# A hybrid retention and delta-rule layer on one core: weights split into high and low parts once and kept in DRAM

## The chip, the cores and the metric

The kernel runs on one core of a Trainium2 chip. Its engines are TensorE (PE, matrix products), VectorE (DVE), ScalarE (ACT), GpSimd (POOL) and SyncE (SP, which issues most of the DMAs). The metric is the device time of one execution in microseconds, as the median of three runs.

## The reference

One layer over 2048 new prompt tokens and 64 sample tokens, with a model width of 1024, in float32. The mixer has four retention heads and four gated delta heads that share one input projection and one output projection; the MLP is a squared ReLU, 4096 wide.

```python
def _layer(x, pos_offset, s_ret, s_gdn, s_conv, pre_mix_w, w_in, ...):
    h = _rmsnorm(x, pre_mix_w)
    m, S_r, S_g, new_conv = _hybrid_mixer(h, pos_offset, s_ret, s_gdn, s_conv, w_in, conv_w, ...)
    x = x + _rmsnorm(m, post_mix_w)
    h = _rmsnorm(x, pre_mlp_w)
    f = jnp.square(jax.nn.relu(jnp.einsum('bld,df->blf', h, w_up)))
    f = jnp.einsum('blf,fd->bld', f, w_down)
    x = x + _rmsnorm(f, post_mlp_w)
    return x, S_r, S_g, new_conv
```

Inside the mixer each head is a recurrence over chunks. For a delta head the kernel inverts a triangular 128 x 128 matrix per chunk, block by block.

## The kernel before

The 2048 prompt tokens go through as four blocks of 512; the 64 sample tokens go along with the second block. Each block has a projection stage (16 units of weights), the heads, an output projection (4 units of `w_out`), and an MLP in eight groups of two units of `w_up` and two of `w_down`. The weights do not stay in SBUF: every block reads all of them from DRAM, 52 units of four pieces, so 208 pieces a block and 832 in all. A piece is 128 partitions x 512 numbers, 256 KB (264 KB for `w_vg0`).

A float32 product is made from three products of a rounded 32-bit form that PE runs fast: high x high, high x low, low x high. So each piece is split after its load (`load_unit`, L339 to L354): ACT copies it into the rounded form (`whi`, through the helper at L248), and DVE or POOL subtracts this from the original (`wlo`, helper L254). The tuple `pool=(1, 1, 0, 0)` gives the first two pieces of a unit to POOL and the last two to DVE. There are five buffers `wraw` for raw pieces (RB) and six each for `whi` and `wlo` (WB); a buffer is used again in turn when its last reader is done.

There are two kinds of products. In `gemm_fm` (projections, `w_up`) the weights are the stationary operand, and a unit is passed through once for each of its two column groups. In `gemm_tm` (`w_vg`, `w_out`, `w_down`) the tokens are stationary, and a unit is passed through once for each of the four tiles of 128 tokens. In `w_out` the contraction goes in the order 0, 4, 1, 5, 2, 6, 3, 7 of the heads' outputs.

The order of work on PE is written by the program: a class (`Weave`) interleaves the main stream of products with side streams, such as the heads, from a table of assumed latencies, and PE keeps that order. From the second block on, the projections of a block are woven together with the MLP of the block before it; the last block's MLP runs alone at the end. On the other engines and on SP's queue, a scheduler sets the order when the program is built. Each engine, and SP's queue of DMAs too, takes its instructions strictly in order.

A delta head sends parts of its matrix through small DMAs on SP's queue: `XX<-ym` and `ym<-ym` (L789, L782, L783) before the inversion of the 16 x 16 blocks, `ym<-xf` (L808 to L811) after it, and `ym<-ym` (L824) after the joining of pairs of blocks. Each waits for DVE.

Of the kernel before, what the change touches and what calls it, by code (L numbers as in the profile page):

```python
# [8 lines left out]
F32 = mybir.dt.float32  # L9
F32R = mybir.dt.float32r  # L10
# [18 lines left out]
NF = 4  # L29
# [92 lines left out]
class Weave:  # L122
    """Interleaves the main stream of matrix products with side streams whose
    steps wait on other engines; keeps an estimate of the tensor engine's clock."""
# [54 lines left out]
    def merge(self, *gens):  # L179
        """Units of the streams given, the earlier stream first where it is ready.  # L180
        A stream yields a tuple of keys before each unit, and None within it."""
        todo = [[next(g), g] for g in gens]
        while todo:
            for e in todo:
                if self.ready(e[0]):
                    break
            else:
                yield [e[0] for e in todo]
                continue
            while True:  # L190
                try:
                    x = next(e[1])
                except StopIteration:
                    todo.remove(e)
                    break
                if isinstance(x, tuple):
                    e[0] = x
                    break
                yield x
# [3 lines left out]
def hybrid_kernel(ctx: ExitStack, tc: tile.TileContext, I, O, NB: int, SB: int):  # L203
# [13 lines left out]
    mmp = ctx.enter_context(tc.tile_pool(name="mmp", bufs=MMB, space=PS))  # L217
    drp = ctx.enter_context(tc.tile_pool(name="drp", bufs=2, space=bass.MemoryType.DRAM))
# [53 lines left out]
    # ---- constants  # L272
# [65 lines left out]
    # ---- weights: streamed pieces, split into hi + lo  # L338
    def load_unit(src, n, ncol):  # L339
        """src: [128, n, ncol] in DRAM; returns accessors k -> AP [128, ncol] for hi and lo."""  # L340
        per = 2 if ncol <= NU else 1
        his, los = [], []
        for q in range(n // per):
            fit = lambda t: t[:, :per * ncol].rearrange("p (a c) -> p a c", a=per)
            r = fit(page([P, 2 * NU], "wraw", bufs=RB))
            nc.sync.dma_start(r, src[:, per * q:per * (q + 1), :])
            hi = fit(page([P, 2 * NU], "whi", F32R, bufs=WB))
            lo = fit(page([P, 2 * NU], "wlo", F32R, bufs=WB))
            act(hi, r, AF.Copy)
            tt(lo, r, hi.bitcast(F32), ALU.subtract, eng=(V, G)[TUNE["pool"][q % 4]])  # L350
            his.append(hi)
            los.append(lo)
        return (lambda k: his[k // per][:, k % per, :]), (lambda k: los[k // per][:, k % per, :])

    def gemm_tm(ps, a, wu, c0, rows, ks, first=True, last=True):
        """ps[rows, :] (+)= a[:, ks, c0:c0+rows]^T W[ks], in three passes."""
        ahi, alo = a
        whi, wlo = wu
        ks = list(ks)
        for n, k in enumerate(ks):  # L360
            lh, ll = ahi[:, k, c0:c0 + rows], alo[:, k, c0:c0 + rows]
            matmul(ps, lh, whi(k), start=(first and n == 0), stop=False)
            matmul(ps, lh, wlo(k), start=False, stop=False)
            matmul(ps, ll, whi(k), start=False, stop=(last and n == len(ks) - 1))
            if n % 2 == 1:
                yield

    def gemm_samp(wd, a, wu):
        """Sample rows of a, times W: rows of the high parts, then rows of the low parts, added up."""
        ps = mm()  # L370
        whi, wlo = wu
        for k in range(KT):
            both = a[0][:, k, T:T + 2 * NS]
            matmul(ps[:, :wd], both, whi(k), start=(k == 0), stop=False)
            matmul(ps[:, :wd], both, wlo(k), start=False, stop=(k == KT - 1))
            if k % 2 == 1:
                yield
        x = page([P, 512], "fs")[:NS, :wd]
        V.tensor_copy(x, ps[NS:2 * NS, :wd])
        tt(x, x, ps[:NS, :wd], ALU.add)  # L380
        return x

    def gemm_fm(ps, a, wu, m, n0, n1):
        """ps[128, n1-n0] = W[:, 128m:128m+128]^T a[:, :, n0:n1]."""
        ahi, alo = a
        whi, wlo = wu
        for k in range(KT):
            wh, wl = whi(k)[:, m * P:(m + 1) * P], wlo(k)[:, m * P:(m + 1) * P]
            matmul(ps, wh, ahi[:, k, n0:n1], start=(k == 0), stop=False)
            matmul(ps, wh, alo[:, k, n0:n1], start=False, stop=False)  # L390
            matmul(ps, wl, ahi[:, k, n0:n1], start=False, stop=(k == KT - 1))
            yield
# [4 lines left out]
    class Block:  # L397
# [23 lines left out]
        # ------------ input norm  # L421
        def place(self):
            """high and low parts; with the sample rows, their low parts once more behind the high ones"""
# [3 lines left out]
        def prep_first(self):  # L427
# [15 lines left out]
            self.w0 = load_unit(I["w_vg0"], KT, NU)  # L443
# [80 lines left out]
        # ------------ mixer output: kept in DRAM until the operand's place is free  # L524
# [33 lines left out]
        # ------------ gates of the delta heads  # L558
# [70 lines left out]
        # ------------ gated delta heads  # L629
        def conv_channel(self, ct, pss, out, outs, raws):  # L630
            """pre-conv projections in PSUM -> silu(conv) in out [128, T] and outs [128, NS]."""
# [38 lines left out]
        def spare(self, i, h):  # L670
            """places that only the first block has, for its odd heads"""
# [6 lines left out]
        def proj_qk(self, h):  # L678
            kq = self.spare(0, h) or page([P, 2, T], "kq", bufs=2)
            kqs = small([P, 2, NS], "kqs") if self.samp else None  # L680
            wu = load_unit(I["w_qk"][h], KT, UNIT)
# [5 lines left out]
        def proj_vz(self, h):  # L687
            vz = self.spare(1, h) or page([P, 2, T], "Ss" if self.b == 0 and h else "vz")
            vzs = small([P, 2, NS], "vzs") if self.samp else None
            wu = load_unit(I["w_vz"][h], KT, UNIT)  # L690
# [16 lines left out]
        def gdn_head(self, h):  # L707
# [12 lines left out]
            # decay matrix  # L720
# [7 lines left out]
            # token-major k and q  # L728
# [33 lines left out]
            # (k k^T o D)^T | (q k^T o D)^T, rows weighted by c  # L762
# [6 lines left out]
            # diagonal blocks of 16: one block a partition, rows of the inverse in turn  # L769
# [35 lines left out]
            # pairs of blocks: (T1^T M21^T) T2^T, four rows a partition, zero for the second block's  # L805
# [25 lines left out]
            # token-major v  # L831
# [5 lines left out]
            # T = (I + M C)^-1 by doubling  # L837
# [18 lines left out]
            # recurrence over chunks  # L856
# [148 lines left out]
        # ------------ retention heads  # L1005
# [8 lines left out]
        def ret_place(self, h):  # L1014
            """four places of [P, 1024]; the first one is free before the others are"""
# [7 lines left out]
        def proj_vg(self, h):  # L1023
# [3 lines left out]
            if h == 0 and b == 0:  # L1027
                wu = self.w0
            else:
                wu = load_unit(I["w_vg0"] if h == 0 else I["w_ret"][h, 1], KT, wd)  # L1030
# [26 lines left out]
        def proj_ret(self, h):  # L1057
# [4 lines left out]
            wu = load_unit(I["w_ret"][h, 0], KT, UNIT)  # L1062
# [99 lines left out]
        # ------------ mixer  # L1162
# [46 lines left out]
        # ------------ output projection, residual, second norm  # L1209
        def out_proj(self, then=None):  # L1210
# [17 lines left out]
            for u in range(4):  # L1228
                wu = load_unit(I["w_out"][u], KT, UNIT)
# [66 lines left out]
        # ------------ MLP  # L1296
# [17 lines left out]
        def mlp_up(self, g):  # L1314
            self.f = f = (page([P, NF, T], "fhi", F32R), page([P, NF, T], "flo", F32R),
                          page([P, NF, 2, NS], "fs", F32R) if self.samp else None)
            for u in range(NF // 2):
                if u:
                    yield ()
                wu = load_unit(I["w_up"][g * (NF // 2) + u], KT, UNIT)  # L1320
# [11 lines left out]
        def mlp_down(self, g, then=None):  # L1332
            if g == 0:
                self.acc = [page([P, D_MODEL], atag[t]) for t in range(self.nt)]
            for u in range(2):
                if u and g < NG - 1:
                    yield ()
                whi, wlo = wu = load_unit(I["w_down"][g, u], NF, T)
# [7 lines left out]
                for t, (c0, rows) in enumerate(self.tiles):  # L1346
# [6 lines left out]
                    else:  # L1353
                        # rows of the high parts, then rows of the low parts; added up at the end
# [162 lines left out]
```

## Time and profile before

| | |
|---|---|
| runs | 3055.93, 3059.34 and 3065.72 us |
| median | 3059.34 us |
| span of the profiled execution | 3047.0 us, the only time of it that is given |
| busy, share of the span | PE 94%, DVE 61%, ACT 38%, POOL 34% |
| mean granted TensorE clock | 0.979 |
| moved by DMA | 317.82 MB, 104 GB/s on the mean |

The profile is one execution. An engine's busy time says how much work it has; whether this work sets the end is said by the waits, which name for each stretch of idleness the instruction that ended it. Numbers such as "31.9, 21, 3.9" in a wait are the time in total, the number of waits, and the longest.

### The profile page before, as it was taken

To read this page: it belongs to the slowest core of one execution; us is meant where nothing else is said; L and a number is where in the kernel's file an instruction comes from. 1 tells how busy PE (TensorE), PEld (TensorE's weight loads), DVE (VectorE), ACT (ScalarE), POOL (GpSimd) and SP (SyncE) were. 2 spreads that over 40 slices of the span, in tenths; PEclk is the share of its full clock that TensorE was granted. 3 is DMA by queue.
4 is the path that set the end of the run, shared out by engine and by line. 5 is a ranking of instruction groups with operands and counts; after the bars stand their busy time and mean duration, and the time that the engine had idled before them with its cause. 6 is when DMAs were issued, how large, how long until landed. Compare 5 with 4: busy or idle time off the path is not lost.

```text
span 3047.0 us, 45242 instructions
## 1 busy us (share of the span) xinstructions
PE 2856.1 (94%) x16072; PEld 2458.0 (81%) x16072; DVE 1871.7 (61%) x3698; ACT 1149.0 (38%) x2823; POOL 1047.3 (34%) x922
## 2 busy tenths in 40 slices
PE   7888989999899998999999999999999999989998
PEld 6777887878788697888888989877878787878886
DVE  6978687475757537764757373677475756543334
ACT  4343533334334334433333333443333343433332
POOL 4332223333333324333323232533243333443333
PEclk9999999999999999999999999999999999999999
DMA  5223432323233225322232332542222232442233
GB/s 180 80 74 99 136 103 83 105 79 119 83 102 118 86 97 172 126 65 94 69 114 75 95 94 93 175 137 75 92 87 90 84 116 82 160 138 94 94 97 108
DMA packets 208195, 317.82 MB, mean 104 GB/s; under 512 B 59744, under 2 KB 68320, under 8 KB 207968
## 3 DMA queue, kind: packets, MB, share of 16 engines
q1 hardware_dynamic: 199056, 286.26, 29.9%
q0 software_dynamic: 7760, 26.56, 2.2%
q8 instruction: 126, 2.06, 0.3%
q10 hardware_dynamic: 1152, 2.10, 0.2%
q14 instruction: 101, 0.83, 0.1%
HBM read 279.35 MB, written 28.67 MB: 101 GB/s over the span
## 4 chain that ended last, share of the span: by engine, by line
PE 37%; DVE 8%; issue 2%; DMA 2%; ACT 1%; POOL 0%; SPq 0%; DVEq 0%; POOLq 0%; ACTq 0%
PE mm L266 34%; PE mx L266 3%; DVE wlo L254 1%; DVE XX L254 1%; DVE ym L254 1%; PE mx L270 1%; DVE mt L254 1%; DMA raw<-x1d 1%; DVE a L251 0%; DMA raw<-in_x_prompt 0%; DVE a L254 0%; DVE r L254 0%; DVE raw L254 0%; DVE flo L254 0%; DVE kv L251 0%
## 5 line engine op out<-in xcount | busy, mean ns | idle before, releaser
L254 POOL TENSOR_TENSOR wlo<-wraw,whi 128x512 fp32r<-128x512 f32 (+1 forms) x416 | 580.2, 1407 | 981.7 <-ACT whi L248 864.6
L248 ACT ACTIVATE whi<-wraw 128x512 fp32r<-128x512 f32 (+1 forms) x832 | 513.6, 629 | 634.5 <-PE mm L266 516.8
L266 PE MATMUL mm<-ahi,whi 128*128 128x512 f32 (+2 forms) x1520 | 561.3, 369 | 5.7 <-ACT raw L248 5.7
L266 PE MATMUL mm<-ahi,wlo 128*128 128x512 f32 (+2 forms) x1520 | 543.8, 358 | 21.7 <-DVE wlo L254 21.7
L266 PE MATMUL mm<-alo,whi 128*128 128x512 f32 (+2 forms) x1520 | 542.3, 357 | 2.1 <-DVE alo L254 2.1
L254 DVE TENSOR_TENSOR wlo<-wraw,whi 128x512 fp32r<-128x512 f32 (+1 forms) x416 | 330.8, 802 | 178.5 <-ACT whi L248 176.3
L266 PE MATMUL mm<-whi,fhi 128*128 128x512 f32 x1024 | 416.8, 407 | 17.9 <-DVE a L254 10.5
L266 PE MATMUL mm<-wlo,fhi 128*128 128x512 f32 x1024 | 410.1, 401 | 19.8 <-DVE wlo L254 17.7
L266 PE MATMUL mm<-whi,flo 128*128 128x512 f32 x1024 | 408.8, 399 | 15.3 <-DVE flo L254 15.1
L266 PEld LDWEIGHTS mm<-ahi,wlo 128*128 128x128 f32 x1520 | 290.2, 191 | 66.1 <-DVE wlo L254 25.5
L266 PEld LDWEIGHTS mm<-ahi,whi 128*128 128x128 f32 x1520 | 291.6, 192 | 46.4 <-issue 6.6
L266 PEld LDWEIGHTS mm<-alo,whi 128*128 128x128 f32 x1520 | 291.4, 192 | 35.9 <-DVE alo L254 2.5
L266 PE MATMUL mm<-bhi,whi 128*128 128x512 f32 (+2 forms) x768 | 277.3, 361 | 2.1 <-ACT raw L248 2.1
L266 PE MATMUL mm<-bhi,wlo 128*128 128x512 f32 (+2 forms) x768 | 266.7, 347 | 1.5 <-DVE r L259 0.8
L266 PE MATMUL mm<-blo,whi 128*128 128x512 f32 (+2 forms) x768 | 267.3, 348 | 0.0
L254 POOL TENSOR_TENSOR raw<-raw 128x512 f32<-128x512 f32 (+2 forms) x166 | 156.8, 945 | 309.7 <-ACT fhi L248 218.7
L266 PEld LDWEIGHTS mm<-wlo,fhi 128*128 128x128 f32 x1024 | 195.5, 191 | 70.3 <-DVE wlo L254 27.8
L266 PEld LDWEIGHTS mm<-whi,fhi 128*128 128x128 f32 x1024 | 195.4, 191 | 66.3 <-DVE a L254 14.5
L266 PEld LDWEIGHTS mm<-whi,flo 128*128 128x128 f32 x1024 | 195.1, 191 | 64.3 <-DVE flo L254 20.6
L266 PE MATMUL mm<-whi,bhi 128*128 128x256 f32 (+1 forms) x832 | 236.9, 288 | 3.1 <-DVE raws L647 1.8
L254 DVE TENSOR_TENSOR a<-a,mm 128x512 f32<-128x512 f32 x224 | 151.5, 682 | 139.4 <-PE mm L266 139.0
L248 ACT ACTIVATE raw<-mm 128x512 f32<-128x512 f32 (+2 forms) x226 | 113.5, 503 | 317.5 <-PE mm L266 268.6
(498 smaller groups left out, 5179.6 us busy)
## 6 DMA issues: line engine op xcount, KB each, us to landing
wraw<-in_w_up SPq DMA_DIRECT2D x256, 256.0 KB
wraw<-in_w_down SPq DMA_DIRECT2D x256, 256.0 KB
wraw<-in_w_ret SPq DMA_DIRECT2D x112, 256.0 KB
wraw<-in_w_vz SPq DMA_DIRECT2D x64, 256.0 KB
wraw<-in_w_qk SPq DMA_DIRECT2D x64, 256.0 KB
wraw<-in_w_out SPq DMA_DIRECT2D x64, 256.0 KB
raw<-in_x_prompt SPq DMA_DIRECT2D x32, 256.0 KB
mixd<-raw POOLq DMA_DIRECT2D x24, 256.0 KB, 3.1
```

The source lines that it names most:

```text
L248: return A.activation(out, in_, f, **kw)
L254: return (eng or V).tensor_tensor(out=out, in0=a, in1=b, op=op)
L266: return tc.keep_in_program_order(nc.tensor.matmul(out, lhsT, rhs, start=start, stop=stop))
L270: return tc.keep_in_program_order(nc.tensor.transpose(out, in_, ident[:rows, :rows]))
```

## The change

`load_unit` now takes the name and index of a unit. The first time that a unit is asked for, which is always in the first block, it does as before, and writes high and low parts of each piece, 512 KB, into a tile in DRAM (`ws`), with a DMA on SP's queue. Each later time it reads this tile straight into the pair of parts. High and low part now share one buffer `wpc` of twice the size; there are six of them. The raw buffers `wraw` stay, for the first block and for other loads that used them already.

```diff
+    wst = ctx.enter_context(tc.tile_pool(name="wst", bufs=1, space=bass.MemoryType.DRAM))
...
-    def load_unit(src, n, ncol):
...
+    stored = {}
+
+    def load_unit(name, idx, n, ncol):
+
+        src = I[name]
+        for i in idx:
+            src = src[i]
         per = 2 if ncol <= NU else 1
+        w = per * ncol
+        first = (name, idx) not in stored
+        if first:
+            stored[name, idx] = [wst.tile([P, 2 * w], F32, tag=nm("ws"), name=nm("ws")) for q in range(n // per)]
         his, los = [], []
         for q in range(n // per):
-            fit = lambda t: t[:, :per * ncol].rearrange("p (a c) -> p a c", a=per)
-            r = fit(page([P, 2 * NU], "wraw", bufs=RB))
-            nc.sync.dma_start(r, src[:, per * q:per * (q + 1), :])
-            hi = fit(page([P, 2 * NU], "whi", F32R, bufs=WB))
-            lo = fit(page([P, 2 * NU], "wlo", F32R, bufs=WB))
-            act(hi, r, AF.Copy)
-            tt(lo, r, hi.bitcast(F32), ALU.subtract, eng=(V, G)[TUNE["pool"][q % 4]])
+            fit = lambda t: t.rearrange("p (a c) -> p a c", a=per)
+            both = page([P, 4 * NU], "wpc", F32R, bufs=WB)
+            hi, lo = fit(both[:, :w]), fit(both[:, w:2 * w])
+            if first:
+                r = fit(page([P, 2 * NU], "wraw", bufs=RB)[:, :w])
+                nc.sync.dma_start(r, src[:, per * q:per * (q + 1), :])
+                act(hi, r, AF.Copy)
+                tt(lo, r, hi.bitcast(F32), ALU.subtract, eng=(V, G)[TUNE["pool"][q % 4]])
+                if NB > 1:
+                    nc.sync.dma_start(stored[name, idx][q], both[:, :2 * w].bitcast(F32))
+            else:
+                nc.sync.dma_start(both[:, :2 * w].bitcast(F32), stored[name, idx][q])
             his.append(hi)
             los.append(lo)
...
-            wu = load_unit(I["w_qk"][h], KT, UNIT)
+            wu = load_unit("w_qk", (h,), KT, UNIT)
...
-                whi, wlo = wu = load_unit(I["w_down"][g, u], NF, T)
+                whi, wlo = wu = load_unit("w_down", (g, u), NF, T)
```

The order of the matmuls on PE is the same in both programs. What follows shows three places on the other queues. Line numbers of the new program are 13 to 15 higher from `load_unit` on.

SP's queue in the last block, at the second delta head (tiles `ym` and `XX` are that head's). Before:

```order
L346 DMA wraw_22509<-in_w_down 128x512
L808 DMA ym_22215<-xf 128x1x64
L809 DMA ym_22215<-xf 128x1x256
L811 DMA ym_22215<-xf 128x1x16 x4
L346 DMA wraw_22515<-in_w_down 128x512
L346 DMA wraw_22584<-in_w_down 128x512
L346 DMA wraw_22590<-in_w_down 128x512
L346 DMA wraw_22596<-in_w_down 128x512
L824 DMA ym_22215<-ym_22215 128x1x16 x4
L346 DMA wraw_22602<-in_w_down 128x512
```

The same place now, where `ws_8574` to `ws_8577` are the four pieces that were `wraw_22497` to `wraw_22515`, the first unit of a group of `w_down`:

```order
L365 DMA wpc_21137<-ws_8455 128x1024
L823 DMA ym_20953<-xf 128x1x64
L824 DMA ym_20953<-xf 128x1x256
L826 DMA ym_20953<-xf 128x1x16 x4
L365 DMA wpc_21139<-ws_8456 128x1024
L365 DMA wpc_21141<-ws_8457 128x1024
L365 DMA wpc_21203<-ws_8574 128x1024
L365 DMA wpc_21205<-ws_8575 128x1024
L839 DMA ym_20953<-ym_20953 128x1x16 x4
L365 DMA wpc_21207<-ws_8576 128x1024
```

The head's last shuffle stood ahead of the fourth piece of the second unit, and stands now ahead of the third piece of the first: five pieces earlier in the stream of weights.

POOL at the same head; `raw` is a square for the MLP's low parts, `ym` belongs to the head. Before:

```order
L254 TENSOR_TENSOR raw_22462<-raw_22462 128x512
L254 TENSOR_TENSOR wlo_22587<-wraw_22584,whi_22586 128x512
L254 TENSOR_TENSOR wlo_22593<-wraw_22590,whi_22592 128x512
L254 TENSOR_TENSOR ym_22215<-mt_22206,cst 128x512
L254 TENSOR_TENSOR raw_22492<-raw_22492 128x512
L254 TENSOR_TENSOR wlo_22700<-wraw_22697,whi_22699 128x512
```

And now:

```order
L255 TENSOR_TENSOR raw_21130<-raw_21130 128x512
L255 TENSOR_TENSOR raw_21168<-raw_21168 128x512
L255 TENSOR_TENSOR ym_20953<-mt_20944,cst 128x512
L255 TENSOR_TENSOR raw_21198<-raw_21198 128x512
L255 TENSOR_TENSOR ym_20953<-mt_20944,cst 128x512
```

The low parts are gone; the square still stands behind the head's `ym`.

SP's queue at the very start, loads of the tokens (`a`, and transposed `fhi`, `flo`) and constants. Before:

```order
L437 DMA a_13_122<-in_x_prompt 128x512 x2
L440 DMA flo_125<-in_xpT 128x8x128
L437 DMA a_14_123<-in_x_prompt 128x512 x2
L440 DMA flo_125<-in_xpT 128x8x128
L317 DMA cst<-in_cst 128x1032
```

And now:

```order
L452 DMA a_13_124<-in_x_prompt 128x512 x2
L455 DMA flo_127<-in_xpT 128x8x128
L452 DMA a_14_125<-in_x_prompt 128x512
L363 DMA ws_138<-wpc_142 128x1056
L452 DMA a_14_125<-in_x_prompt 128x512
L455 DMA flo_127<-in_xpT 128x8x128
L363 DMA ws_139<-wpc_148 128x1056
L363 DMA ws_140<-wpc_154 128x1056
L363 DMA ws_141<-wpc_160 128x1056
L318 DMA cst<-in_cst 128x1032
```

The stores of the first unit (`ws`) stand between and behind the loads of the tokens, and ahead of the constants.

## Rows read from the trace of the kernel before

**Rows 1.** The page: busy time, share of the span, instructions; bytes moved by DMA.

```profile
PE 2856.1 (94%) x16072; PEld 2458.0 (81%) x16072; DVE 1871.7 (61%) x3698; ACT 1149.0 (38%) x2823; POOL 1047.3 (34%) x922
...
DMA packets 208195, 317.82 MB, mean 104 GB/s; under 512 B 59744, under 2 KB 68320, under 8 KB 207968
```

**Rows 2.** Waits of PE from 1066 us on: us in total, times, longest.

```profile
PE mm L266 <- DVE wlo L254: 31.9, 21, 3.9
PE mx L270 <- DVE mt L254: 18.7, 8, 4.4
PE mm L266 <- DVE flo L254: 8.4, 7, 2.6
PE mm L266 <- DVE a L254: 7.3, 7, 2.2
...
PE mm L266 <- ACT whi L248: 3.2, 2, 2.0
```

**Rows 3.** Waits of PE from 376 to 1066 us.

```profile
PE mx L270 <- DVE mt L254: 11.3, 4, 5.0
PE mm L266 <- DVE wlo L254: 8.2, 7, 2.7
PE mm L266 <- DVE flo L254: 6.7, 5, 2.9
```

**Rows 4.** Groups by shape: busy us, mean ns; idle before them, releasers.

```profile
L254 POOL TENSOR_TENSOR wlo<-wraw,whi 128x512 fp32r<-128x512 f32 x408 | 568.7, 1407 | 959.7 <-ACT whi L248 857.8 <-DVE wlo L254 43.1 <-DVE gp L254 15.4
L248 ACT ACTIVATE whi<-wraw 128x512 fp32r<-128x512 f32 x816 | 503.3, 629 | 625.3 <-PE mm L266 512.2 <-issue 72.1 <-DMA wraw<-in_w_ret 10.1
...
L254 DVE TENSOR_TENSOR wlo<-wraw,whi 128x512 fp32r<-128x512 f32 x408 | 325.2, 804 | 178.5 <-ACT whi L248 176.3 <-PE mm L266 0.4
```

**Rows 5.** Instructions on tile wlo: ns min/median/max, first and last start.

```profile
L254 POOL TENSOR_TENSOR wlo<-wraw,whi x416: 1260/1299/3537, 8.7 to 3014.6; 128x512 fp32r<-128x512 f32 x136, 128x528 fp32r<-128x528 f32 x3
L254 DVE TENSOR_TENSOR wlo<-wraw,whi x416: 668/692/1796, 11.8 to 3025.0; 128x512 fp32r<-128x512 f32 x136, 128x528 fp32r<-128x528 f32 x3
```

**Rows 6.** DMA issues: count, KB each, median us from issue to landing.

```profile
mixd<-raw POOLq DMA_DIRECT2D x24, 256.0 KB, 3.1
...
out_y_p<-a POOLq DMA_DIRECT2D x12, 512.0 KB, 4.9
...
out_ret_s<-Ss POOLq DMA_DIRECT2D x4, 512.0 KB, 3.5
```

**Rows 7.** Timeline of ACT and PE at two handovers: start us, us, what.

```profile
2605.88 1.15 ACT L248 ACTIVATE whi<-wraw 128x512 fp32r<-128x512 f32 x2 [0.54 <-PE mm L266]
...
2607.08 0.28 PE L266 MATMUL mm<-whi,bhi 128*128 128x256 f32 x1
2607.20 0.28 PE L266 MATMUL mm<-wlo,bhi 128*128 128x256 f32 x1
...
2712.80 2.70 ACT L248 ACTIVATE whi<-wraw 128x512 fp32r<-128x512 f32 x4 [7.48 <-PE mm L266]
...
2712.60 0.40 PE L266 MATMUL mm<-whi,fhi 128*128 128x512 f32 x1
2712.84 0.39 PE L266 MATMUL mm<-wlo,fhi 128*128 128x512 f32 x1
```

**Rows 8.** Stretches: us, busy us of PE, PEld, DVE, ACT, POOL, PEclk, DMA share, GB/s.

```profile
0.00:376.00 376.00, 323.56 (x1943) 284.75 (x1944) 293.64 (x673) 161.72 (x455) 119.64 (x101) 0.95 0.36 112
...
1066.00:1250.00 184.00, 172.44 (x1040) 152.85 (x1039) 105.69 (x177) 72.57 (x176) 73.76 (x70) 0.96 0.43 141
```

**Rows 9.** Second delta head of the last block: timeline of DVE and SP, chain.

```profile
2236.26 2.38 DVE L254 TENSOR_TENSOR wlo<-wraw,whi 128x512 fp32r<-128x512 f32 x2
...
2258.41 0.69 DVE L822 TENSOR_REDUCE ym<-ym 128x32 f32<-128x512 f32 x1
...
2250.56 1.83 SPq L346 DMA_DIRECT2D wraw<-in_w_down  x4
2259.12 2.53 SPq L824 DMA_DIRECT2D ym<-ym  x4
...
2254.94 3.47 PE mm L266 x15
```

**Rows 10.** Waits of PE from 2690 us on, all there are.

```profile
PE mm L266 <- ACT raw L248: 5.2, 1, 5.2
```

More of the change, by code (lines that the diff above doesn't have):

```diff
@@ L442, in prep_first @@
             load(0)
-            self.w0 = load_unit(I["w_vg0"], KT, NU)
+            self.w0 = load_unit("w_vg0", (), KT, NU)
             for t in range(1, NC):
@@ L689, in proj_vz @@
             vzs = small([P, 2, NS], "vzs") if self.samp else None
-            wu = load_unit(I["w_vz"][h], KT, UNIT)
+            wu = load_unit("w_vz", (h,), KT, UNIT)
             pss = yield from self.proj_fm(wu, 1)
@@ L1029, in proj_vg @@
             else:
-                wu = load_unit(I["w_vg0"] if h == 0 else I["w_ret"][h, 1], KT, wd)
+                wu = load_unit(*(("w_vg0", ()) if h == 0 else ("w_ret", (h, 1))), KT, wd)
             if h == 0:
@@ L1061, in proj_ret @@
             nc.sync.dma_start(rt, I["rope"][:, :, b * T:(b + 1) * T])
-            wu = load_unit(I["w_ret"][h, 0], KT, UNIT)
+            wu = load_unit("w_ret", (h, 0), KT, UNIT)
             qk = get(2).rearrange("p (a i) -> p a i", a=2)
@@ L1228, in out_proj @@
             for u in range(4):
-                wu = load_unit(I["w_out"][u], KT, UNIT)
+                wu = load_unit("w_out", (u,), KT, UNIT)
                 if u == 1 and then:
@@ L1319, in mlp_up @@
                     yield ()
-                wu = load_unit(I["w_up"][g * (NF // 2) + u], KT, UNIT)
+                wu = load_unit("w_up", (g * (NF // 2) + u,), KT, UNIT)
                 if g == 0 and u == 0:
```

## Prediction

> **What bounds the kernel now.** I read the page first. PE is busy 94% of a span of 3047.0 us, DVE 61%, ACT and POOL about a third each [rows 1]. PE runs its instructions in a fixed order, so the kernel gets shorter only where PE stands still, and longer wherever PE gets a new wait. What is to be had is the idle 6%, 191 us, and only the part of it that weights cause.
>
> The waits of PE by stretch say how much that is. From 1066 us on, when the first block's MLP is over and every weight would come from the scratch, PE waits 31.9 us for the low parts on DVE and 3.2 us for the high parts on ACT [rows 2]. Between 376 and 1066 us, where the first block's MLP and the second block's projections are woven together, it waits 8.2 us for low parts [rows 3]. The other waits are for results of DVE: mt (rotary embedding), flo (low parts of the MLP's hidden layer) and a (accumulators): 34.4 us after 1066 us [rows 2], and mt and flo 18.0 us before it [rows 3]. The groups by shape give the price of the splitting: 1407 ns on POOL, 629 ns on ACT and 804 ns on DVE a piece [rows 4]. That is much work, but PE seldom waits for it.
>
> **What goes.** 624 of 832 pieces are no longer split: 312 low parts on POOL (312 x 1.407 = 439 us), 312 on DVE (251 us), 624 high parts on ACT (392 us). None of these sums is on the path. What PE gets back directly is 31.9 + 3.2 us, and of the 8.2 us I count 3 for the second block: **-38 us**.
>
> Indirectly, DVE and POOL answer sooner. The mt, flo and a waits are 52 us. A part of each is the chain itself: in the third quarter of the fourth block POOL's square `raw` stands behind a `ym` that waits for DVE, and it stands behind it in the new order too. Lower bound 0, upper bound 52; I take half, **-25 us**, since two of the low parts, 0.7 us each, often stand in front of such a step [rows 5].
>
> **What comes in: the refill.** Before, a piece is loaded into one of five raw buffers, and only then split into one of six pairs. When PE lets go of a pair, the next piece lies in SBUF, and it is ready after 0.63 + 0.80 us (ACT, DVE) or 0.63 + 1.41 us (ACT, POOL). After, the load itself goes into the pair, so that it can start only when PE has let go, and the raw buffers are of no use any more. The lead falls from eleven pieces to six, and the latency of a refill from 1.4 to 2.0 us rises to that of a 512 KB transfer. Rows for 512 KB give 3.5 us (a quiet stretch) and 4.9 us (a busy one); 256 KB takes 3.1 us [rows 6]. A load of 4 KB rows in a mostly quiet stretch is nearest to the first: I take 3.8.
>
> The Trainium skill, "DMA: Bandwidth & Descriptors", section "Anatomy of one DMA", gives 2.0 us plus the bytes over 436 GB/s, which is an estimate of 3.2 us here; the 3.5 and 4.9 us of the rows are above it. By it the refill term below would be 22 us and not 45.
>
> How long has a refill? Units have four pieces, so with six buffers the third and fourth piece of a unit take the places of the first and second of the unit before. The pitch of matmuls is 0.23 us for 512 columns and 0.117 us for 256 [rows 7].
> - w_down, first to second unit, where they adjoin: from the last use of piece 1 to the first use of the next unit's piece 3 there are 9 + 6 matmuls, 15 x 0.23 = 3.5 us. ACT starts four high parts in a row at 2712.80, at the moment when PE lets go of the first [rows 7]. Two loads start 0.7 us apart; at 112 GB/s for a share of 0.36 [rows 8] the engines move about 311 GB/s when full, 1.7 us for 512 KB, so that the second lands about 0.9 us later than it would by itself: 3.8 + 0.9 - 3.5 = 1.2 us. 17 such pairs adjoin in PE's order (8 of them in the last block), 20 us.
> - w_out: the contraction runs in the order 0, 4, 1, 5, ..., and 18 matmuls x 0.117 = 2.1 us lie between. 3.8 - 2.1 = 1.7 us, three times in each of three blocks, 15 us. ACT starts the high parts there at 2605.88, right at PE's release [rows 7].
> - The second block has units in halves of 256 and 320 columns and a fifth row tile, with 2.6 to 4.0 us at some twelve places: 12 x 0.8 = 10 us.
>
> Elsewhere (up after up, projections) 4.7 to 7 us lie between and the refill is hidden; when the queue is late this cover is gone (next part). Sum **+45 us**; with 3.1 us for a load 18, with 4.9 us 87.
>
> **What comes in: SP's queue.** SP issues in order, and the delta heads send their small shuffles (L789, L782, L808, L811, L824) through it, each waiting for DVE. Before, weights behind such a wait had eleven pieces of lead. At the second head of the last block, DVE ends the reduction at 2259.10, SP issues the four shuffles until 2261.65, and before them it had loaded down to piece 3 of the second w_down unit [rows 9]. After, the next load in the queue behind that wait is piece 3 of the first unit, which PE reaches 6 matmuls after 2258.4 [rows 9], at about 2259.8. It would land at 2261.65 + 3.8 = 2265.5: a wait of 5.7 us, if DVE comes to the shuffle no earlier. It does come earlier, since four low parts stood on DVE in that head's chain, two of them at 2236.26 for 2.38 us [rows 9]; that leaves 2 to 3 us at a bad place and nothing at others. For twelve heads I take 1.8 us each, **+22 us**. Below: 0. Above: 12 x 5.7 = 68.
>
> **What comes in: traffic.** Per block 54.5 MB of weights; written once as 109 MB, and read three times as 109 instead of 54.5 MB. 318 MB [rows 1] become about 318 + 109 + 164 = 591 MB, 193 GB/s. At the start the first block's 80 projection and output pieces add 42 MB in 376 us, 112 GB/s on 112 GB/s, a share of 0.72 instead of 0.36 [rows 8]. A store waits for the same split as the raw load five pieces on, so it holds SP little; the first four stores stand between the loads of x, 4 x 1.7 us of transfer, half of which I count as late, some 3 us. At the handover of blocks (1066 to 1250 us: 0.43 at 141 GB/s [rows 8]) residual rows, x and weights meet; twice the traffic would be 0.86. I take **+10 us** for both; below 0, above 40, if some 25 refills wait for one more piece, 1.6 us, each.
>
> **Sum.** 3047.0 - 38 - 25 + 45 + 22 + 10 = 3061 us of span. The median of the runs shown, 3059.34 us, is 12.3 us above the span of the profiled execution, which has no other time of its own; so 3073 us, 0.5% slower. A measurement of this kernel can tell about 0.3%, that is 9 us, from no change.
>
> **Rivals.**
> 1. Relief wins (faster). The split work delays DVE more than the waits tell: low parts on DVE take from 668 to 1796 ns with a median of 692, and on POOL 1260 at least [rows 5], so one on DVE sometimes loses 1.1 us, about as long as an instruction of POOL. If most of the 52 us went (-50), DVE's shuffles came early enough (+4), loads took 3.5 us (+33) and traffic cost 5: 3047 - 38 - 50 + 33 + 4 + 5 = 3001, 3013 us. It decides when relief and removed waits together exceed refill and queue. For it: DVE is the engine that PE waits for most. Against it: from 2690 us on the last block's MLP runs alone with all its splitting, and PE's list holds one wait, which is not for weights [rows 10], so there the change can only cost. The Trainium skill, "SBUF — State Buffer", section "SBUF: two separate sides", says that a DVE operation with two SBUF inputs and a GpSimd operation lock each other out for a whole instruction; the spread above agrees with that, and by that rule this rival would be the forecast.
> 2. It cancels (within 0.3%): the same terms with a load of 3.5 us and 12 us for the queue, 3047 - 38 - 25 + 33 + 12 + 10 = 3039, 3051 us.
> 3. The queue's full price (much slower): DVE comes no earlier, +68, loads take 4.9 us because two or three are always under way, +70, traffic +25: 3047 - 38 - 25 + 68 + 70 + 25 = 3147, 3159 us. For it: refills come in pairs, and each is twice as large. Against it: a share of about 0.6 leaves gaps.
>
> That the change does nothing is excluded: the low parts are gone from POOL's order.
>
> **Chances.** Forecast (slower by 0.3 to 1.7%) 0.40; rival 3 0.13; rival 2 0.17; rival 1 0.30. Faster 0.30, same 0.17, slower 0.53. The range leaves out a little of rival 1 and most of rival 3: 3018 to 3130; the forecast's own is 3060 to 3112.
>
> **What would show it.** Busy time of POOL near 610, ACT near 757, DVE near 1600 us. PE's waits for low parts after 1066 us gone, and instead waits for DMA of the weight pages, 60 to 75 us in all; 1.2 us each at the eight w_down pairs of the last block, whose stretch from 2690 us to the end becomes some 8 us longer; 1.7 us at the nine handovers of w_out; single waits of 2 to 6 us behind shuffles. DMA near 590 MB. I am wrong if PE's waits for these DMAs are under 35 us, if the waits for mt, flo and a fall by much more than 25 us, or if the first 376 us change by over 15 us.

## The result and the profile after

| | before | after |
|---|---|---|
| median of the runs on the same chip | 3060.95 us (4 runs) | 3096.62 us (4 runs, 3088.47 to 3100.63) |
| ratio | | 1.0118, 95% interval 1.0099 to 1.0137 |
| profiled execution: time, span | span 3047.0 us | 3096.51 us, span 3094.7 us |

The change makes the kernel 1.2% slower; 0.5% was forecast. Of the time of the profiled execution after, 1.8 us lie around its span. So the 12.3 us that the prediction added to the span of before were mostly not around it: that execution was a quick one, some 12 us under the median. Differences of spans below (+47.7 us in all) hold these 12 us, the difference of the medians (+35.7 us) does not; in which stretches they lie is not known.

The page after, engines and bytes, which answers to [rows 1]:

```profile
PE 2864.7 (93%) x16072; PEld 2456.4 (79%) x16072; DVE 1552.2 (50%) x3386; ACT 793.0 (26%) x2199; POOL 603.0 (19%) x610
...
DMA packets 238130, 590.49 MB, mean 191 GB/s; under 512 B 63072, under 2 KB 71648, under 8 KB 237920
```

DVE lost 319 us of work, ACT 356, POOL 444, and the kernel got longer all the same: but for the 43 us of waits in [rows 2, 3], that work was not on the path. PE's idle time grew from 191 us to 230, its busy time by 8.6 us; together this is the 47.7 us. The bytes came out as forecast (591 MB).

The waits of PE after, over the whole span (us in total, times, longest), which answer to [rows 2, 3]; `mm` are results of the main stream of products, `mx` those of the side streams:

```profile
PE mm L267 <- DMA wpc<-ws: 96.2, 89, 5.6
PE mx L271 <- DVE XX L255: 23.6, 5, 10.1
PE mx L271 <- DVE mt L255: 12.2, 12, 1.5
PE mm L267 <- DVE a L255: 8.9, 6, 2.5
...
PE mm L267 <- DVE flo L255: 8.0, 5, 3.1
...
PE mm L267 <- ACT wpc L249: 5.4, 3, 3.0
...
PE mm L267 <- DVE wpc L255: 4.8, 6, 1.5
```

The waits for split parts that remain are nearly all in the first block. In their place stands one new line, the first: 96.2 us for loads from the scratch. Four rows of matmuls take nearly all of them (moving operand, stationary operand; busy us, mean ns; idle before, releasers):

```profile
L267 PE MATMUL mm<-ahi,wpc 128*128 128x512 f32 (+2 forms) x3040 | 880.3, 364 | 38.1 <-DMA wpc<-ws 32.6 <-ACT raw L249 2.9 <-ACT wpc L249 1.1
L267 PE MATMUL mm<-wpc,fhi 128*128 128x512 f32 x2048 | 665.5, 406 | 47.9 <-DMA wpc<-ws 31.9 <-DVE a L255 8.9 <-DVE r L1275 4.0
...
L267 PE MATMUL mm<-bhi,wpc 128*128 128x512 f32 (+2 forms) x1536 | 428.0, 353 | 11.9 <-DMA wpc<-ws 9.4 <-ACT raw L249 2.5
...
L267 PE MATMUL mm<-wpc,bhi 128*128 128x256 f32 (+1 forms) x1664 | 301.2, 286 | 23.5 <-DMA wpc<-ws 22.2 <-ACT bhi L249 1.1
```

`w_up` and the projections of `gemm_fm` (the first and third row) wait 42.0 us, `w_down` (second) 31.9, `w_out` with a few projections of `gemm_tm` (last) 22.2. The first and the third row by shape:

```profile
L267 PE MATMUL mm<-ahi,wpc 128*128 128x512 f32 x1824 | 621.8, 405 | 9.8 <-DMA wpc<-ws 5.8 <-ACT raw L249 1.6 <-ACT wpc L249 1.1
...
L267 PE MATMUL mm<-ahi,wpc 128*128 128x256 f32 x704 | 144.0, 291 | 28.0 <-DMA wpc<-ws 26.8 <-ACT raw L249 1.1
...
L267 PE MATMUL mm<-bhi,wpc 128*128 128x256 f32 x384 | 84.9, 296 | 9.4 <-DMA wpc<-ws 9.4
```

Of the 42.0 us, 36.2 are in matmuls of 256 columns: the second block, whose 576 tokens go through in halves of 256 and 320 columns.

Since PE's order is the same in both kernels, the start of the same matmul can be compared. Cut at seven such matmuls, the 47.7 us lie here (the last column is the part of the 96.2 us in that stretch):

| before, us | after, us | longer by | waits for scratch loads |
|---|---|---|---|
| 0 to 385, first block's mixer | 0 to 403 | +18 | 2.9 |
| 385 to 1066 | 403 to 1086 | +2 | 8.0 |
| 1066 to 1276, end of the second block's mixer, `w_out` | 1086 to 1304 | +8 | 10.8 |
| 1276 to 1876 | 1304 to 1908 | +4 | 24.4 |
| 1876 to 2030, `w_out` and handover | 1908 to 2080 | +18 | 21.6 |
| 2030 to 2590 | 2080 to 2626 | -14 | 12.4 |
| 2590 to 2733, `w_out` and handover | 2626 to 2773 | +4 | 12.1 |
| 2733 to 3047, last block's MLP alone | 2773 to 3094.7 | +7 | 4.0 |

So two kinds of places lose most: the first block's mixer, where next to nothing is read from the scratch yet, and the stretches around `w_out`; the last block's MLP alone loses 7 us. I read the fourth and the sixth stretch as relief and refill against each other.

What a refill takes is read from the chain of waits. Four stretches of it after, in order of time (start us, us, what):

```profile
1963.94 3.09 PE mm L267 x27
1967.03 7.37 DMA wpc<-ws
...
2279.82 0.61 SPq L797
...
2280.53 3.55 DMA wpc<-ws
2284.08 0.04 issue
2284.12 2.07 PE mm L267 x4
...
2663.95 4.04 PE mm L267 x35
2667.99 3.69 DMA wpc<-ws
...
2748.77 3.23 PE mm L267 x14
2752.00 0.02 issue
2752.02 4.96 DMA wpc<-ws
```

At 2667.99 us (a handover of `w_out`) and at 2752.02 us (a pair of `w_down` units) the load follows directly on PE's last use of the page: pure refill, 3.69 us in a quiet place and 4.96 us as one of four loads in a row. At 1967.03 us, a handover of blocks, it takes 7.37 us. At 2280.53 us the load stands behind the shuffles of a delta head on SP. The 89 waits can be sorted by the time between PE's release of a page (its last use in PE's order) and SP's issue of the load. 72 follow a load that SP issued within 0.7 us of the release; they hold 67% of the time, 65 of the 96.2 us. Five follow one behind rows of x or of the residual (18%, 17 us), ten one behind shuffles (13%, 13 us), two are left. The five loads behind rows were issued only 0.9 to 1.9 us late, so that the queue explains at most 5 of their 17 us.

### The profile page after: what moved, and what is told of

Its sections match the earlier page's. It is cut to its first block, busy times and chain, and to the rows that moved or that the text cites. A ratio compares the mean times of both kernels' runs of the same rounds, so it can differ in the third digit from the quotient of the medians.

```text
span 3094.7 us, 43223 instructions
## 1 busy us (share of the span) xinstructions
PE 2864.7 (93%) x16072; PEld 2456.4 (79%) x16072; DVE 1552.2 (50%) x3386; ACT 793.0 (26%) x2199; POOL 603.0 (19%) x610
## 4 chain that ended last, share of the span: by engine, by line
PE 65%; DMA 14%; DVE 13%; issue 2%; SPq 2%; ACT 2%; POOL 1%; DVEq 0%; POOLq 0%; ACTq 0%
PE mm L267 57%; DMA wpc<-ws 8%; PE mx L267 7%; PE mx L271 2%; DVE ym L255 1%; DVE XX L255 1%; DVE mt L255 1%; DVE raw L255 1%; ACT junk L249 1%; DVE wpc L255 1%; DMA wraw<-in_x_prompt 1%; DVE XX L252 1%; DMA raw<-in_x_prompt 1%; DMA ym<-xf 1%; DMA ym<-ym 1%
## 5 line engine op out<-in xcount | busy, mean ns | idle before, releaser
L267 PE MATMUL mm<-ahi,wpc 128*128 128x512 f32 (+2 forms) x3040 | 880.3, 364 | 38.1 <-DMA wpc<-ws 32.6
L267 PE MATMUL mm<-wpc,fhi 128*128 128x512 f32 x2048 | 665.5, 406 | 47.9 <-DMA wpc<-ws 31.9
L267 PEld LDWEIGHTS mm<-ahi,wpc 128*128 128x128 f32 x3040 | 547.8, 191 | 127.9 <-DMA wpc<-ws 39.6
L267 PE MATMUL mm<-alo,wpc 128*128 128x512 f32 (+2 forms) x1520 | 540.4, 355 | 1.4 <-DVE alo L255 1.4
L267 PEld LDWEIGHTS mm<-wpc,fhi 128*128 128x128 f32 x2048 | 381.2, 192 | 150.7 <-DMA wpc<-ws 45.2
L267 PE MATMUL mm<-bhi,wpc 128*128 128x512 f32 (+2 forms) x1536 | 428.0, 353 | 11.9 <-DMA wpc<-ws 9.4
L267 PE MATMUL mm<-wpc,flo 128*128 128x512 f32 x1024 | 410.3, 401 | 8.0 <-DVE flo L255 8.0
L267 PE MATMUL mm<-wpc,bhi 128*128 128x256 f32 (+1 forms) x1664 | 301.2, 286 | 23.5 <-DMA wpc<-ws 22.2
L267 PEld LDWEIGHTS mm<-alo,wpc 128*128 128x128 f32 x1520 | 290.6, 191 | 34.4 <-DVE alo L255 1.6
L267 PEld LDWEIGHTS mm<-bhi,wpc 128*128 128x128 f32 x1536 | 274.6, 190 | 46.2 <-DMA wpc<-ws 11.6
L267 PEld LDWEIGHTS mm<-wpc,flo 128*128 128x128 f32 x1024 | 196.2, 192 | 56.3 <-DVE flo L255 10.8
```

The costliest lines, as they stand in the source:

```text
L267: return tc.keep_in_program_order(nc.tensor.matmul(out, lhsT, rhs, start=start, stop=stop))
```

## The experiments

Three theories were tested for the 96 us. **A, lead**: a page is refilled only when PE lets go of it, and six pages leave about as much time as a 512 KB load takes. **B, queue**: loads are issued late, because SP stands behind other waits. **C, traffic**: with twice the bytes every transfer is slow. All ratios are to the kernel before, run on the same chip.

### More and fewer pages

**Seven pages** (e1).

```diff
-    WB = 6
-    RB = 5
+    WB = 7
+    RB = 3
```

> Seven weight pages instead of six, paid for with two of the five raw buffers, which only the first block fills with weights; nothing else changes. Theory A (refill latency at a short lead: a load starts when PE lets go, and the time to its use is about as long as its landing): one page more is 12 matmuls, 2.8 us, more for each load, so PE's waits for weight DMAs fall from 96 us to 30 to 45 us and the time to 3030 to 3050 us, ratio to the kernel before 0.990 to 0.998; the first 403 us may become 0 to 8 us longer with fewer raw buffers. Theory B (SP's queue: loads are late because SP stands behind other waits, for 5 us and more at a time): waits of 2 to 6 us stay, the sum stays at 60 us or more, ratio 1.002 to 1.008. Theory C (traffic: transfers themselves are slow because twice the bytes move): waits stay at 80 us or more, ratio 1.008 or more.

Measured: 1.0018 (1.0007 to 1.0030). Waits of PE, whole span, and the stretch of the first block that suffers (us, busy us of PE, PEld, DVE, ACT, POOL, granted clock, DMA share, GB/s):

```profile
PE mm L267 <- ACT wpc L249: 27.6, 8, 6.6
PE mm L267 <- DMA wpc<-ws: 22.8, 19, 4.8
```

```profile
330.00:403.00 73.00, 57.65 (x367) 52.84 (x368) 36.90 (x85) 25.24 (x78) 9.50 (x8) 0.81 0.47 160
```

One page more takes 73 of the 96 us away, though the same bytes move through the same queue: theory A, and beyond the 30 to 45 us left that I had given it. The ratio misses A's range and lies next to B's, because two raw buffers less hurt the first block far more than I expected: it ends 46 us later than before (the kernel after: 20), and PE now waits 27.6 us for high parts. From there on this kernel wins 41 us on before.

**Five pages** (e9).

```diff
-    WB = 6
+    WB = 5
```

> The changed kernel with five weight pages instead of six: the suspected cost made larger. Theory A (lead): each load has 2.8 us less; a quarter of the loads had 5.5 us or less from PE's release to the first use, by the order of PE's matmuls, and now have 2.7 us or less against landings of 3.6 to 4.9 us, so some 150 loads wait 1 to 2 us each: waits for weight DMAs 96 us to 200 to 350 us, time 3180 to 3330 us. Theory B (SP's queue) and C (traffic): waits grow by less than half, time under 3140 us.

Measured: 3319.49 us, one run, span 3317.7 us; clock 0.960 against 0.978 in the kernel after. Page and waits:

```profile
PE 2965.6 (89%) x16072; PEld 2503.0 (75%) x16072; DVE 1556.0 (47%) x3386; ACT 793.0 (24%) x2199; POOL 603.5 (18%) x610
```

```profile
PE mm L267 <- DMA wpc<-ws: 230.5, 217, 5.3
```

Both within A's numbers and far outside those of B and C.

**Eight pieces of lead, first block untouched** (e5). The raw buffers that stand idle after the first block hold every fourth piece.

```diff
+            turn[0] += 1
+            apart = not first and turn[0] % 4 == 0
+            if apart:
+                hi, lo = (fit(page([P, 2 * NU], "wraw", F32R, bufs=RB)[:, :w]) for i in range(2))
+            else:
+                both = page([P, 4 * NU], "wpc", F32R, bufs=WB)
+                hi, lo = fit(both[:, :w]), fit(both[:, w:2 * w])
...
+            elif apart:
+                nc.sync.dma_start(hi.bitcast(F32), fit(stored[name, idx][q][:, :w]))
+                nc.sync.dma_start(lo.bitcast(F32), fit(stored[name, idx][q][:, w:2 * w]))
```

> As the changed kernel, with six weight pages and five raw buffers, but in the later blocks every fourth piece goes into two of the raw buffers that stand idle there (its high and its low part as two loads of 256 KB), so that the lead is eight pieces and the first block is as in the changed kernel. Theory A (lead): waits for weight DMAs 96 us to 10 to 25 us; the first block's growth of 14 to 20 us stays; from there on 30 to 45 us are won on the kernel before, as the seven pages won after their slow first block: span 3018 to 3035 us, ratio 0.989 to 0.996. Theory B (traffic): DMA moves as much as before, waits over 50 us, ratio 1.000 or more.

Measured: 0.9928 (0.9905 to 0.9951), span 3026.5 us. Waits of PE:

```profile
PE mx L271 <- DVE mt L255: 14.3, 12, 3.1
...
PE mm L267 <- DMA wraw<-ws: 7.0, 3, 3.7
PE mm L267 <- DVE flo L255: 6.8, 5, 2.0
...
PE mm L267 <- DMA wpc<-ws: 5.5, 2, 3.9
```

The waits for scratch loads are down to 12.5 us, though as many bytes (590.53 MB) move, through the same queue. This version beats both kernels. By the same matmuls it is 22 us behind before when the first block's MLP ends, and 22 us ahead at the end: 44 us won on three blocks.

### The loads themselves

**High parts only** (e2).

```diff
-                nc.sync.dma_start(both[:, :2 * w].bitcast(F32), stored[name, idx][q])
+                nc.sync.dma_start(hi.bitcast(F32), fit(stored[name, idx][q][:, :w]))
...
-            los.append(lo)
+            los.append(lo if first else hi)
```

> Only the high parts are loaded from the scratch (256 KB a piece instead of 512), and PE uses them in place of the low parts too, so that its instructions stay as many; part of the computation is left out, the loads and what follows from their size are what is measured. Stores in the first block as in the changed kernel. Theory A: a load lands in some 3.3 us instead of 4.9, refills that start at PE's release are mostly in time, waits for weight DMAs fall from 96 to 30 to 45 us, ratio 0.990 to 0.997. Theory B (SP's queue): size matters little, waits stay at 65 us or more, ratio 1.003 or more. Theory C (traffic): the same as A for the later blocks, and in addition residual loads and shuffles land sooner; waits under 25 us, ratio under 0.990.

Measured: 0.9878 (0.9862 to 0.9894); waits:

```profile
PE mm L267 <- DMA wpc<-ws: 40.2, 34, 4.5
```

The waits are in A's range and the ratio just under it, in C's. With six pages and a load of half the size most waits are gone, so it is lead against duration of a load; whether a load is long for its own bytes or for the others in flight, this run does not tell.

**w_out and w_down split on the fly** (e4).

```diff
+        own = name in ("w_out", "w_down")
...
-            if first:
+            if first or own:
```

> w_out and w_down are split on the fly in every block as before, and only w_up and the projections come from the scratch. In the changed kernel about 61 us of the 96 us of waits for weight DMAs are for w_down and w_out. Theory A: those 61 us go, some 12 us of waits for split pieces come back and a third of the relief (9 us) is lost, the first block's stores are 40% fewer (6 us): 3097 - 61 + 12 + 9 - 6 = 3051 us, ratio 0.994 to 1.000, waits for weight DMAs 25 to 40 us. Theory B (SP's queue at handovers of blocks and behind shuffles): loads of raw pieces now share the queue with five raw buffers of lead, but the waits of w_up (37 us) stay and the late ones of w_down move to its raw loads only in part: 3060 to 3075, ratio 1.000 to 1.005.

Measured: 0.9971 (0.9957 to 0.9985), waits for scratch loads 50.7 us (43 times). The ratio is A's; the waits are more than A said, since what is left for `w_up` and the projections still has six pages.

### SP's queue

**Shuffles issued by ACT** (e6): in the seven `dma_start` calls of L797 to L839, as here:

```diff
-            nc.sync.dma_start(m2, prod[:nb, :BB * BB].unsqueeze(1).to_broadcast([nb, P // nb, BB * BB]))
+            nc.scalar.dma_start(m2, prod[:nb, :BB * BB].unsqueeze(1).to_broadcast([nb, P // nb, BB * BB]))
```

> As the changed kernel, but the delta heads' small shuffles are issued from ACT's queue, so that no weight load stands behind one that waits for DVE. If the queue term of the prediction is real: the single waits of 1 to 2.5 us behind shuffles go, waits for weight DMAs 96 us to 74 to 84 us, ratio 1.004 to 1.008, if ACT, which is busy a quarter of the time, bears the waiting. If the loads there are late because of their lead and landing alone: 90 us or more, ratio 1.010 or more.

Measured: 1.0320 (1.0298 to 1.0343). Waits of PE:

```profile
PE mm L267 <- DMA wpc<-ws: 84.4, 82, 5.5
PE mm L267 <- DVE flo L255: 26.7, 7, 6.7
...
PE mm L267 <- DVE fhi L252: 11.0, 1, 11.0
...
PE mx L271 <- ACT kSs L249: 10.2, 2, 10.0
```

The waits for loads fall by 11.8 us, which is what the sorting above gives to shuffles (13). As a remedy it fails: the waits moved to ACT come back in `flo`, `fhi` and `kSs`.

**Residual rows issued by ACT** (e7): `nc.sync` becomes `nc.scalar` in L1281 and L1424.

```diff
-                nc.sync.dma_start(x, self.x1d[c0:c0 + rows, cols])
+                nc.scalar.dma_start(x, self.x1d[c0:c0 + rows, cols])
```

> As the changed kernel, but the rows of x and of the first residual (the loads into raw in the norms, which wait for DVE to free one of two buffers) are issued from ACT's queue. Six waits at the handovers of blocks, 5.8, 5.1, 4.9, 4.0, 2.7 and 1.8 us, follow a weight load that stands right behind such a load in SP's queue. If the queue is their cause: 15 to 24 us less, ratio 1.004 to 1.007. If they come from slow landings (6 to 7.4 us there, many transfers at once): under 6 us less, ratio 1.009 or more.

Measured: 1.0144 (1.0122 to 1.0166), waits for scratch loads 88.4 us. 7.8 us less, between the two expectations, and no time won. With the 5 us of lateness above, the waits at the handovers of blocks come mainly from landings of 6 to 7 us, and only in part from the queue.

### The first block

**Stores without reads** (e3).

```diff
-            if first:
+            if True:
...
-                if NB > 1:
+                if first and NB > 1:
```

> The first block stores its pieces as in the changed kernel, but the later blocks never read them: they split on the fly as before (one page per piece in place of two tiles). What is left is the price of the stores in the first block. If the stores cost what the first 403 us of the changed kernel suggest, the first block gets 14 to 20 us longer and the rest is as before: 3070 to 3085 us, ratio 1.003 to 1.008. If the growth there came from the reads of the second block's weights that begin at 360 us, 0 to 6 us: ratio 1.000 to 1.002.

Measured: 1.0064 (1.0044 to 1.0085). **The same with half the bytes** (e8).

```diff
-                    nc.sync.dma_start(stored[name, idx][q], both[:, :2 * w].bitcast(F32))
+                    nc.sync.dma_start(stored[name, idx][q][:, w:], both[:, w:2 * w].bitcast(F32))
```

> The first block stores only the low parts (256 KB a piece instead of 512; the store waits for the same split) and the later blocks split on the fly, as in the run that only stored. With both parts stored the kernel took 1.0064 times the time before. If bytes are the price of the stores: half of it, 1.002 to 1.004. If the place of the stores in SP's queue is the price: as much, 1.005 to 1.008.

Measured: 1.0049 (1.0032 to 1.0066), which decides nothing. What both share is the page for both parts, so it was tried by itself: **one page, no scratch** (e12), the kernel before with

```diff
-            hi = fit(page([P, 2 * NU], "whi", F32R, bufs=WB))
-            lo = fit(page([P, 2 * NU], "wlo", F32R, bufs=WB))
+            both = page([P, 4 * NU], "wpc", F32R, bufs=WB)
+            hi, lo = fit(both[:, :w]), fit(both[:, w:2 * w])
```

> The kernel before, with one change: a piece's high and low parts share one page, as in the changed kernel, in place of two tiles; nothing is stored and nothing is read from a scratch. The run that only stored (1.0064) had both this page and the stores, and half the bytes cost as much (1.0049). If the stores are the price: ratio 0.999 to 1.001 here, first 385 us within 3 us of before. If the shared page is (a page comes free, or is waited for, only as a whole): 1.003 to 1.007, and the first 385 us get longer by 8 to 16 us.

Measured: 1.0021 (1.0008 to 1.0034), between the two expectations: about 6 us for the shared page, which leaves 0.43%, 13 us, for the stores (0.28% with half the bytes). The two intervals leave 6 to 20 us for the 13. The traces agree with this only up to the first block's mixer: at the matmul that starts at 385 us before, e12 is 6.4 us late (again between the expectations), e3 11.3, the kernel after 17.5. At 1066 us it is 14.3 us for e12, without any store, 14.7 for e3 and 20.2 for the kernel after.

**Stores issued by POOL, with eight pieces of lead** (e10).

```diff
-                    nc.sync.dma_start(stored[name, idx][q], both[:, :2 * w].bitcast(F32))
+                    nc.gpsimd.dma_start(stored[name, idx][q], both[:, :2 * w].bitcast(F32))
```

> Eight pieces of lead as in the run before, and the stores of the first block issued from POOL's queue instead of SP's. That run lost 17 to 22 us in the first block and took 0.9928 of the time before. If the loss comes from the stores' place in SP's queue (shuffles, x and raw pieces behind a store that waits for a split): 8 to 18 us of it come back, ratio 0.987 to 0.990. If it comes from the bytes in the DMA engines: as before, 0.991 to 0.994. If POOL, which computes a quarter of the time there, suffers from the waits of its stores: 0.994 or more.

Measured: 1.0024 (1.0010 to 1.0039), against 0.9928 with SP. What POOL waits for, its stores being line 369:

```profile
POOL ws L369 <- DVE wpc L255: 141.8, 50, 11.7
```

POOL stands in front of its own work until DVE has split the next piece; the third expectation came true.

**Projections never stored, with eight pieces of lead** (e11): as e5, and

```diff
+        own = name in ("w_vg0", "w_ret", "w_qk", "w_vz")
+        first = own or (name, idx) not in stored
...
-                if NB > 1:
+                if NB > 1 and not own:
```

> Eight pieces of lead, but the projections (w_vg, w_ret, w_qk, w_vz) are split on the fly in every block and never stored; the scratch holds w_out, w_up and w_down. The first block's mixer has no stores then: the 12 to 17 us that the first 376 us lost come back, of the rest of the first block's growth 5 us stay; in the later blocks 3 x 60 pieces, 29% of those that the scratch had spared, are split again, which gives back some 10 us of waits for low parts and of relief. Span 3027 - 14 + 10 = 3023 us, ratio 0.988 to 0.994. If splitting of the projections is what the other waits hang on: 0.995 or more.

Measured: 0.9915 (0.9893 to 0.9936), the ratio as forecast, and not to be told from e5; the span of the profiled execution, 3033.9 us, is 11 us over the forecast. At the matmul that starts at 314.7 us before, it is 5 us behind before, e5 12 us; when the first block's MLP ends, 18 us against 22. Whether the MLP's stores, which remain, cost the difference to 5 us is not shown, since e12 without stores is 14 us behind there.

## Why the prediction was right, and which terms were mis-sized

The sign and the mechanism were right: the removed work was not on PE's path, and the lead of prefetching was paid for it. The time, 3096.6 us, is in the forecast's own range (3060 to 3112) and 23.6 us above its value; the slowdown, 35.7 us by the medians, is 2.6 times the 13.7 us that were forecast. So the range covers a sum that was too small. Term by term, span against span:

| term | forecast | measured |
|---|---|---|
| waits for split parts that go | -38 | -42: the 31.9 and 3.2 us of [rows 2] all gone, 8.2 us of [rows 3] now 1.4 |
| relief of mt, flo, a | -25 | -26: mt 30.0 to 12.2, flo 15.1 to 8.0, a 10.5 to 8.9 |
| refill | +45 | +65 |
| SP's queue behind shuffles | +22 | +13 (12 by e6) |
| traffic at handovers, and start | +10 | +17 at handovers, +18 in the first block's mixer |
| sum | +14 | +45 of 47.7 |

**Removed waits and relief** were right to a few us. The Trainium skill, "SBUF — State Buffer", section "SBUF: two separate sides", has a DVE operation with two SBUF inputs and a GpSimd operation lock each other out; the traces agree with it. GpSimd lost 42% of its busy time, and many of DVE's operations on two SBUF tiles became quicker on the mean, here the same 43 before and after:

```profile
L254 DVE TENSOR_TENSOR blo<-wraw,bhi 128x512 fp32r<-128x512 f32 x43 | 34.9, 829 | 2.3 <-ACT bhi L248 2.1
...
L255 DVE TENSOR_TENSOR blo<-wraw,bhi 128x512 fp32r<-128x512 f32 x43 | 30.0, 722 | 1.5 <-ACT bhi L249 1.4
```

`a<-a,mm`, whose second input is an accumulator in PSUM, stayed at 682 and 684 ns. Of DVE's 3698 instructions before, 297 took over 1.1 times the median of their kind, and 296 of these overlap one of POOL in time, as only 1265 of the 3698 do; what they took over their medians fell from 228 to 112 us. So DVE lost 319 us of busy time where the forecast counted 251. That relief is real, but PE had little use for it: the faster rival needed 50 us of PE's waits and got 26.

**The refill** is the step that failed in size: 65 us for 45. `w_down` from unit to unit holds 17 us of it (20 forecast), `w_out` from unit to unit 18 (15); of these, the nine handovers that the prediction names wait 1.4 to 2.1 us each, 16.1 us in all. The term that was mis-sized is "The second block has units in halves of 256 and 320 columns and a fifth row tile, with 2.6 to 4.0 us at some twelve places: 12 x 0.8 = 10 us": there 26 waits hold 25 us of refill, at more than twice as many places and 1.0 us each. The other 5 us are for projections of `gemm_tm` and the first units of `w_out`. "Elsewhere (up after up, projections) 4.7 to 7 us lie between and the refill is hidden" held: the 5.8 us of the 512-column units above all stand behind shuffles, which the prediction put into its next term.

"A load of 4 KB rows in a mostly quiet stretch is nearest to the first: I take 3.8" is true at the handovers of `w_out` (3.69 us in the chain). But a load is 4.96 us as one of four in a row, and 6 to 7.4 us beside rows of x and of the residual; the median of all 612 issue-to-landing times of 512 KB loads, worked out from SP's issues and the queue's semaphore events, is 4.9 us. (The prediction has 87 us for this term with 4.9 us for a load, and 70 in its third rival for the same 4.9; neither changes the forecast.) The estimate of 3.2 us from the Trainium skill, "DMA: Bandwidth & Descriptors", section "Anatomy of one DMA", is 0.5 us under the 3.69 us and 4.2 us under the slowest in the chain above, 7.37 us; the Trainium skill gives that formula for the GpSimd path, and these loads are issued by SP. Transfers are slower in the kernel after, with 191 GB/s moved on the mean instead of 104, also where the change does not touch them: `mixd`, 256 KB from POOL's queue, now lands in 4.7 us instead of the 3.1 of [rows 6].

```profile
mixd<-raw POOLq DMA_DIRECT2D x24, 256.0 KB, 4.7
```

The 1.2 us at each pair of `w_down` units was met at 2757 us (1.12 us), but from 2773 us on no wait is over 0.5 us. The stretch is 7 us longer as forecast (8), by 4.0 us of waits and 3.7 us of busier PE; the sum was right for half the reason.

**SP's queue** was over-sized: ten waits stand behind shuffles, with loads that are 1.0 to 3.7 us late, not 5.7.

**The first block** came to the edge of one of the prediction's own conditions for being wrong, a change of over 15 us in the first 376 us: it is 14.7 us at that matmul and 17.5 at 385 us. "A store waits for the same split as the raw load five pieces on, so it holds SP little" left out that the edit also joins two tiles into one page, which I had costed at nothing: 6 us by e12, and 13 us for the stores by e3, as medians. How the stores cost this, and whether any of it falls after 385 us, is not settled: half the bytes save less than can be told, and taking them off SP made POOL wait. The waits for `XX` (12.9 us before, 23.6 after), at the end of a delta head's shuffles, do not follow the stores: they are 18.7 us in e12, without stores, 26.4 in e11, without stores in the mixer, and 9.5 in e8, with them.

## What to carry to other kernels

When split or converted data is cached and re-read, the landing buffer becomes the working buffer: count the lead in pieces before and after, and the time of a refill in the busiest place, not in a quiet one. Here one page more or less moved the waits from 96 to 23 or 231 us, so room for it should be found first; the raw buffers that the cache makes idle were enough to turn 1.2% slower into 0.7% faster. Work taken off engines that PE seldom waits for paid little here: 1120 us less on DVE, ACT and POOL took 68 us of waits off PE.

## What was not expected of the hardware

Where PE waited more, it was also slower. With five pages (one run) PE waits 134 us longer for loads than with six, and its busy time grows by 101 us for the same 16072 matmuls; the granted clock of the whole span falls from 0.978 to 0.960, that is (twice the share that is missing, times the span) from some 136 to 265 us at 1.2 instead of 2.4 GHz. At half the speed these 129 us more can explain, as an estimate, at most 65 of the 101 us; what the rest is stays open. With seven pages and three raw buffers the clock was 0.81 between 330 and 403 us, where PE was busy 57.65 of 73 us; in the kernel after it was 0.95 there, with 63.95 us busy. So many short waits cost more than their sum in that run.
